# Hymba layer, second sweep: 32x32 vector transposes and a pass through DRAM in place of PE transposes for the keys of 14 chunks

## The chip, the core and the metric

The kernel runs on one core of one Trainium2 chip. The metric is the device time of one execution in microseconds (us). Engines are called PE (TensorE, matrix products), DVE (VectorE), ACT (ScalarE), POOL (GpSimd) and SP (SyncE, whose queue issues nearly all DMA transfers here). The on-chip memories are SBUF (128 partitions) and PSUM, where PE writes.

## The reference

One encoder layer on a sequence of 2048 rows of width 1024, in float32. One input projection feeds two groups of heads; their outputs are put side by side, go through one output projection, and a LayerNorm closes the layer. What the change touches is the second group, attention with compressed queries and keys:

```python
h = x @ w_in                        # split: GLA q,k,v,gate,ranks | c_q (256), c_kv (128), k_rope (64), gate
q  = (rms_norm(c_q,  q_norm_g)  @ w_uq ).reshape(B, S, 4, 128 + 64)
kv = (rms_norm(c_kv, kv_norm_g) @ w_ukv).reshape(B, S, 4, 128 + 128)
q_nope, q_rope = q[..., :128] * scale, apply_rope(q[..., 128:]) * scale
k_nope, v = kv[..., :128], kv[..., 128:]
k_r = apply_rope(k_rope)            # one rotary key for all heads
s = q_nope . k_nope + q_rope . k_r  # per head, 2048 x 2048
o = softmax(s) @ v
out = layer_norm(alpha * x + concat(gla * silu(gate_a), o * silu(gate_b)) @ w_out)
```

The first group is a gated linear attention with a forward and a backward scan over chunks of 64 rows.

## The kernel before

**Split products.** Each float32 operand is kept as a high part (a rounding copy to fp32r, `hi`, L353, mostly on ACT) and a low part (the difference, `lo`, L359, on DVE or POOL). A product is three matmuls: high by high, high by low, low by high (`mm3`, L407 to L409).

**Stages.** The sequence is cut into 16 chunks of 128 rows. A first sweep goes over the chunks from the last to the first and makes the projections of the linear attention and its backward scan (to about 340 us). The second sweep (`sweep_c`, about 359 to 589 us) goes forward in 8 steps of two chunks each. Then comes attention over 16 blocks (4 heads by 4 groups of 512 queries), and the output projection with the LayerNorm.

**The second sweep.** For each chunk PE makes `ipm` (c_q, c_kv and the rotary key); DVE and ACT make the RMS factor (`rm_t` to `rm_r`); ACT writes the normed `cq` and `ckv`, and high and low parts of `ckv` are kept as values, `vh` (ACT) and `vl` (POOL). The rotary key is made as `krs`, high and low halves of 64 columns side by side. The forward scan's output of the chunk is `Ob`, to which the first sweep's part `oib` is added; from it `rg_t` to `rg_r` make the norm's factor, `og` (DVE, with the state product `ub` that SP loads) the gated output, `oT` its transpose on DVE, and four SP transfers store it (`oa_s`). Once per step, PE makes the gates `pz`, from which ACT and DVE make `gm` (stored as `gm_s`), and the absorbed queries `pq`, split into `qah` and `qal` and stored as `qh_s` and `ql_s`; the rotary queries are stored as `rh_s` and `rl_s`. `pz`, `Ob` and `pq` share two PSUM buffers. SP loads the rows of x for a later step as `xcf`, which ACT splits to `xch` and POOL to `xcl`.

**The keys.** Scores need the keys with the feature on the partitions. `c_tm` (L1337 to L1341) transposes four 128x128 pieces per chunk on PE into one PSUM tile `tm`: two of `cq`, one of `ckv`, one of `krs`. From `tm`, ACT writes `ckvT_h` (high part of the transposed `ckv`), DVE writes `ckvT_l` (low part), and ACT writes the transposed `krs`. All three are tiles of 16 chunks that stay in SBUF for attention.

**The order.** Each piece of work of the sweep has a place: a number counted in steps, in tables (`PLACE_C`, `PLACE_C_FIRST` for the first step, `PLACE_C_LAST` for the last). All pieces are sorted by place and issued in that order; `in_order` chains the instructions of each engine, SP's transfers too, so that the order stays as written. Attention's loads are not in this chain: `fetch(i)` (L1515 to L1524) loads the queries of block i as six SP transfers, `qh`, `ql`, twice `rh`, twice `rl`, and a scheduler places those of the first blocks among the sweep's last SP transfers.

**Scores.** For each key tile PE runs five matmuls (L1534 to L1538), all into one PSUM bank:

```python
mm(ps[:, e], kh, qh, start=True, stop=False)
mm(ps[:, e], kh, ql, start=False, stop=False)
mm(ps[:, e], kl, qh, start=False, stop=False)
mm(ps[:, e], kr, rh, start=False, stop=False)
mm(ps[:, e], kr, rl, start=False, stop=True)
```

Here `kh`, `kl` and `kr` are slices of `ckvT_h`, `ckvT_l` and the transposed `krs`.

Of the kernel before, what the change touches and what calls it, by code (L numbers as in the profile page):

```python
# [9 lines left out]
F32 = mybir.dt.float32  # L10
F32R = mybir.dt.float32r
# [7 lines left out]
P = 128  # L19
# [3 lines left out]
NCH = S // P  # L23
# [8 lines left out]
NKT = S // P  # L32
# [97 lines left out]
SETUP_C = ("lset", "u15", "u14", "wS", "wH", "wL", "pb0", "wa0", "wh0", "wl0", "pb1", "wa1", "wh1", "wl1")  # L130
STEP_C = ("gm1", "gm2", "gm3", "gm4", "sgm", "pq", "qah", "qal", "sqa", "sqr")
CHUNK_C = ("lx", "xh", "xl", "lS", "lq", "lo", "lu", "sqm", "ssm", "rml", "rmd", "cq", "ckv", "krf", "krfa",
    "krsh", "krsl", "vh", "vl", "tm", "cqTh", "cqTl", "ckvTh", "ckvTl", "krT", "pqr", "qrf", "qrfa",
    "tq", "qrTh", "qrTl", "Sf1", "Sf2", "M", "Ob", "oib", "sqO",
    "ss", "rgl", "rgd", "og", "oT", "soT")

FETCH_C = ("lx", "xh", "xl")


PLACE_C = dict(  # L140
    ipa=(-0.08, 0.695),
    ipb=(-0.014, 0.701),
    ipc=(0.026, 0.723),
# [2 lines left out]
    tm=(0.532, 1.152),  # L146
    pqr=(0.849, 1.355),
# [6 lines left out]
    cq=(0.519, 1.042),  # L154
    ckv=(0.513, 1.1),
    vh=(0.732, 1.218),
    krsh=(0.45, 0.972),
    cqTh=(0.624, 1.184),
    ckvTh=(0.64, 1.277),
    krT=(0.848, 1.233),  # L160
# [9 lines left out]
    cqTl=(0.758, 1.284),  # L170
    ckvTl=(0.687, 1.321),
    qrf=(0.853, 1.411),
# [6 lines left out]
    krsl=(0.456, 1.044),  # L179
    vl=(0.859, 1.227),  # L180
    qrfa=(0.95, 1.459),
# [30 lines left out]
    wl1=0.556,  # L212
)
PLACE_C_FIRST = dict(
    ipa=(-1.874, 0.381),
    ipb=(-1.582, 0.655),
    ipc=(-0.643, 0.818),
# [2 lines left out]
    tm=(0.445, 1.143),  # L220
    pqr=(0.716, 1.336),
# [6 lines left out]
    cq=(0.33, 1.098),  # L228
    ckv=(0.414, 1.115),
    vh=(0.521, 1.151),  # L230
    krsh=(0.247, 0.988),
    cqTh=(0.547, 1.205),
    ckvTh=(0.483, 1.183),
    krT=(0.871, 1.252),
# [9 lines left out]
    cqTl=(0.579, 1.316),  # L244
    ckvTl=(0.54, 1.33),
    qrf=(0.968, 1.46),
# [6 lines left out]
    krsl=(0.252, 1.09),  # L253
# [89 lines left out]
class K:  # L343
# [145 lines left out]
    def run(self):  # L489
        tc, nc, ins = self.tc, self.nc, self.ins  # L490
        with ExitStack() as top:
            cp = top.enter_context(tc.tile_pool(name="const", bufs=1))
            self.cp = cp
            dp = top.enter_context(tc.tile_pool(name="scr", bufs=1, space=DRAM))
            self.qd_s = [dp.tile([P, H * P], F32, name=f"qd_s{c}") for c in range(NCH)]
            self.oi_s = [dp.tile([P, H * P], F32, name=f"oi_s{c}") for c in range(NCH)]
            self.su_s = [dp.tile([P, H * P], F32, name=f"su_s{c}") for c in range(NCH)]
            self.u_s = [dp.tile([P, H * P], F32, name=f"u_s{c}") for c in range(NCH)]
            self.qa_s = [[dp.tile([P, H, QB], F32, name=f"q{p}_s{b}") for p in "hl"] for b in range(NQB)]
            self.qr_s = [[dp.tile([H, 64, QB], F32, name=f"r{p}_s{b}") for p in "hl"] for b in range(NQB)]  # L500
            self.gm_s = [dp.tile([P, H, QB], F32, name=f"gm_s{b}") for b in range(NQB)]
            self.oa_s = [dp.tile([P, H, P], F32, name=f"oa_s{c}") for c in range(NCH)]
            self.qk_s = [[dp.tile([64, H, P], F32, name=f"{n}_s{c}") for c in range(NCH)] for n in ("qx", "kx")]
            self.r_s = [dp.tile([1, H, QB], F32, name=f"r_s{b}") for b in range(NQB)]
            self.ob_s = [dp.tile([P, H, QB], F32, name=f"ob_s{b}") for b in range(NQB)]

            ident = cp.tile([P, P], F32, name="ident")
            self.ident = ident
            self.gkv_c = cp.tile([P, 1], F32, name="gkv_c")
            self.gn_c = cp.tile([P, 1], F32, name="gn_c")  # L510
            self.cw = cp.tile([P, NCH, 3, H], F32, name="cw")

            psum = ExitStack()
            pspool = lambda n: psum.enter_context(tc.tile_pool(name=n, bufs=2, space=PSUM, reuse_waits="tile"))
            self.gp, self.ip, self.tr = pspool("gp"), pspool("ip"), pspool("tr")
            self.xfp = top.enter_context(tc.tile_pool(name="xfp", bufs=2, reuse_waits="tile"))
            edge = top.enter_context(tc.tile_pool(name="edge", bufs=1, side="right"))
            edge.tile([P, 8], F32, name="edge")
            self.keep = top.enter_context(tc.tile_pool(name="keep", bufs=1, side="right", reuse_waits="tile"))
            wgs = ExitStack()  # L520
            self.wgp = wgs.enter_context(tc.tile_pool(name="wgp", bufs=2 * NK + 1, side="right", reuse_waits="tile"))
            self.xab = wgs.enter_context(tc.tile_pool(name="xab", bufs=2, side="right"))
            self.wgate = []
            self.wl = None
            self.sweep_a()
            self.wz = top.enter_context(tc.tile_pool(name="wz", bufs=2 * NK + 1, reuse_waits="tile"))
            bcs = ExitStack()
            self.wm = bcs.enter_context(tc.tile_pool(name="wm", bufs=2 * NK + 1, reuse_waits="tile"))
            self.bc = bcs.enter_context(tc.tile_pool(name="bc", bufs=1, reuse_waits="tile"))
            self.wl = bcs.enter_context(tc.tile_pool(name="wl", bufs=2, reuse_waits="tile"))  # L530
            self.late_gates()
            wgs.close()
            rp = top.enter_context(tc.tile_pool(name="res", bufs=1, side="right", reuse_waits="tile"))
            self.ckvT_h = rp.tile([P, NKT, P], F32R, name="ckvT_h")
            self.ckvT_l = rp.tile([P, NKT, P], F32R, name="ckvT_l")
            self.kr = rp.tile([P, NKT, P], F32R, name="krs")
            self.vh = rp.tile([P, NKT, P], F32R, name="vh")
            self.vl = rp.tile([P, NKT, P], F32R, name="vl")
            self.sweep_c()
            bcs.close()  # L540
            psum.close()
            self.wof = top.enter_context(tc.tile_pool(name="wof", bufs=PRE_W, side="right", reuse_waits="tile"))
            self.attention()
# [565 lines left out]
    def sweep_c(self):  # L1109


        with ExitStack() as ctx:
            self.w1 = ctx.enter_context(self.tc.tile_pool(name="wk2", bufs=1, reuse_waits="tile"))
            self.sm = ctx.enter_context(self.tc.tile_pool(name="smc", bufs=2, reuse_waits="tile"))
            chunks = [dict(c=c, j=c % 2, st=c // 2) for c in range(NCH)]
            steps = [dict(st=st, ch=chunks[2 * st:2 * st + 2]) for st in range(NCH // 2)]
            for d in chunks:
                d["step"] = steps[d["st"]]
            self.Sf = None
            todo = []  # L1120

            def put(n, st, fn, *a, j=None):
                last = st == len(steps) - 1
                p = PLACE_C[n]
                p = (last and PLACE_C_LAST.get(n)) or (not st and PLACE_C_FIRST.get(n)) or p
                todo.append((st + (p if j is None else p[j]), len(todo), fn, a))

            for n in SETUP_C:
                put(n, 0, getattr(self, "su_" + n))
            for s in steps:  # L1130
                for n in range(8):
                    put("pz", s["st"], self.c_pz, s, n, j=n)
                for n in STEP_C:
                    put(n, s["st"], getattr(self, "c_" + n), s)
            for d in chunks:
                for n in range(4):
                    put("ip" + "abcd"[n], d["st"], self.c_ip, d, n, j=d["j"])
                for n in CHUNK_C:
                    if (d["st"] or n not in FETCH_C) and (d["c"] < NCH - 1 or n not in ("Sf1", "Sf2")):
                        put(n, d["st"], getattr(self, "c_" + n), d, j=d["j"])  # L1140
            last = dict(self.tail)
            for _, _, fn, a in sorted(todo, key=lambda e: e[:2]):
                with self.in_order(last):
                    fn(*a)
# [177 lines left out]
        self.nc.gpsimd.tensor_tensor(d["kr"], d["kr"], d["krt"], ALU.add)  # L1322

    def c_krsh(self, d):
        d["krs"] = self.w1.tile([P, 2, 64], F32R, tag="krs", name=f"krs{d['c']}")
        self.hi(d["krs"][:, 0], d["kr"][:, 0])

    def c_krsl(self, d):
# [5 lines left out]
    def c_vl(self, d):  # L1334
        self.lo(self.vl[:, d["c"]], d["ckv"], self.vh[:, d["c"]], "pool")

    def c_tm(self, d):  # L1337
        tp = d["tm"] = self.tr.tile([P, 4, P], F32, tag="tr", name=f"tm{d['c']}")
        for i, src in enumerate((d["cq"][:, 0:P], d["cq"][:, P:2 * P], d["ckv"],
                                 d["krs"].rearrange("p a d -> p (a d)").bitcast(F32))):  # L1340
            self.nc.tensor.transpose(tp[:, i], src, self.ident)  # L1341

    def c_cqTh(self, d):
        s = d["step"]
# [685 lines left out]
```

## Time and profile before

| what | value |
|---|---|
| time, median of 3 runs | 1277.12 us (1277.00 to 1278.61) |
| the profiled execution's own time | 1277.05 us |
| its span, first to last instruction | 1275.3 us |
| busy: PE / DVE / ACT / POOL | 1251.5 / 898.4 / 732.4 / 720.1 us |
| DMA | 155.24 MB, mean 122 GB/s |

In rows of the profile, "L1341 PE MATMUL tm<-ident,ckv" is the instruction of line 1341 on PE that writes tile `tm` from `ident` and `ckv`. In a timeline the first number is the start in us from the start of the span, the second the duration in us; a bracket holds the idle time of the engine just before, and what ended it. In a tile's rows the three numbers are the shortest, median and longest duration in ns; its last line has the time from the issue of its DMA transfers to their landing in us (shortest, median, longest). SPq is SP's queue: the rows are the issue of transfers. In a row of the windows stand the window, its length, the busy time of each engine with its number of instructions, PE's granted clock, the DMA engines' share and GB/s.

### The profile page before, as it was taken

Reading aid. Unit: us, or ns where it says so; the run is one execution under the profiler, and the core shown is the slowest. Engines: PE = TensorE matmul, PEld = TensorE weight load, DVE = VectorE, ACT = ScalarE, POOL = GpSimd, SP = SyncE. Lnnn points to the kernel's source line nnn. Section 1 sums busy time; section 2 is a strip of 40 time slices with the busy share of each in tenths; the row PEclk is TensorE's granted clock in tenths of the full one; section 3 lists DMA queues with packets and bytes.
Section 4 is the critical chain, followed back from the end, with each engine's and each line's share of the span. In section 5 each row is a group of like instructions: output and inputs, shape, how many; then the busy total and the mean of one; then the engine's idle time right before and its main releaser. Section 6 shows DMA issues by size and latency. Waiting matters only on the chain.

```text
span 1275.3 us, 19650 instructions
## 1 busy us (share of the span) xinstructions
PE 1251.5 (98%) x6986; PEld 1103.4 (87%) x6986; DVE 898.4 (70%) x1601; ACT 732.4 (57%) x1186; POOL 720.1 (56%) x443
## 2 busy tenths in 40 slices
PE   8999999999999999999999999999999999999997
PEld 7999999999899999989788888888888888887886
DVE  6635454544565555554888888888888888479997
ACT  7544444454565544544888888788888888511110
POOL 0132323232345555520598888889999999935541
PEclk9999999999999999999999999999999999999999
DMA  8223434334757777657201111111233110376652
GB/s 292 79 81 110 114 110 115 109 100 114 244 199 205 221 208 206 186 153 219 76 9 49 42 52 52 44 31 58 58 92 91 42 43 10 124 235 195 211 192 99
DMA packets 167233, 155.24 MB, mean 122 GB/s; under 512 B 77046, under 2 KB 119678, under 8 KB 167136
## 3 DMA queue, kind: packets, MB, share of 16 engines
q1 hardware_dynamic: 159072, 151.86, 40.0%
q0 software_dynamic: 672, 2.10, 0.4%
q8 instruction: 55, 0.90, 0.3%
q10 hardware_dynamic: 7392, 0.03, 0.3%
q14 instruction: 42, 0.34, 0.1%
HBM read 100.43 MB, written 53.51 MB: 121 GB/s over the span
## 4 chain that ended last, share of the span: by engine, by line
PE 84%; DVE 5%; DMA 4%; ACT 2%; issue 2%; SPq 2%; POOL 0%; DVEq 0%; ACTq 0%; POOLq 0%
PE pz L1217 7%; PE ipm L1288 5%; PE o L407 4%; PE o L408 4%; PE o L409 4%; PE pS L1534 4%; PE pS L1536 4%; PE pS L1537 4%; PE pS L1538 4%; PE pS L1535 4%; PE ipa L407 4%; PE ipa L409 4%; PE ipa L408 4%; PE ipg L407 2%; PE ipg L408 2%; PE ipg L409 2%
## 5 line engine op out<-in xcount | busy, mean ns | idle before, releaser
L359 POOL TENSOR_TENSOR pl<-s,ph 128x1024 fp32r<-128x1024 f32 x128 | 306.6, 2414 | 53.0 <-ACT ph L353 49.2
L1556 DVE TENSOR_TENSOR rm<-pS,rm 128x512 f32<-128x512 f32 x210 | 144.9, 690 | 35.7 <-ACT s L1543 30.4
L1543 ACT ACTIVATE s<-pS 128x1024 f32<-128x1024 f32 x128 | 131.2, 1025 | 60.6 <-PE pS L1538 51.4
L1580 DVE TENSOR_TENSOR s<-s,mb 128x1024 f32<-128x1024 f32 x128 | 151.2, 1214 | 9.5 <-PE mb L1574 8.8
L353 ACT ACTIVATE ph<-s 128x1024 fp32r<-128x1024 f32 x128 | 135.0, 1056 | 17.2 <-PE o L409 16.5
L1584 ACT ACTIVATE s<-s 128x1024 f32<-128x1024 f32 x128 | 131.3, 1049 | 11.0 <-DVE s L1580 10.9
L407 PE MATMUL ipa<-wah,xah 128*128 128x384 f32 (+1 forms) x384 | 130.1, 339 | 5.1 <-ACT wah L353 5.1
L408 PE MATMUL ipa<-wal,xah 128*128 128x384 f32 (+1 forms) x384 | 124.9, 325 | 0.0
L409 PE MATMUL ipa<-wah,xal 128*128 128x384 f32 (+1 forms) x384 | 124.7, 325 | 0.0
L1534 PE MATMUL pS<-qh,ckvT_h 128*128 128x512 f32 x256 | 102.5, 400 | 0.8 <-DVE rm L1556 0.4
L407 PE MATMUL o<-ph,vh 128*128 128x512 f32 x256 | 101.0, 395 | 0.0
L409 PE MATMUL o<-ph,vl 128*128 128x512 f32 x256 | 99.8, 390 | 0.0
L1537 PE MATMUL pS<-rh,krs 128*128 128x512 f32 x256 | 99.8, 390 | 0.0
L1536 PE MATMUL pS<-qh,ckvT_l 128*128 128x512 f32 x256 | 99.8, 390 | 0.0
L1538 PE MATMUL pS<-rl,krs 128*128 128x512 f32 x256 | 99.7, 389 | 0.0
L1535 PE MATMUL pS<-ql,ckvT_h 128*128 128x512 f32 x256 | 99.7, 389 | 0.0
L408 PE MATMUL o<-pl,vh 128*128 128x512 f32 x256 | 99.7, 389 | 0.0
L1054 POOL TENSOR_TENSOR Sb<-Sb,Us 64x512 f32<-64x512 f32 x15 | 20.9, 1394 | 137.0 <-DVE Us L1046 127.9
L1607 DVE TENSOR_TENSOR ap<-ap,s 128x512 f32<-128x512 f32 x120 | 83.1, 693 | 2.6 <-ACT s L1584 0.7
L407 PEld LDWEIGHTS ipa<-wah,xah 128*128 128x128 f32 x384 | 73.2, 191 | 7.8 <-ACT wah L353 5.5
L359 POOL TENSOR_TENSOR ol<-of,oh 128x512 fp32r<-128x512 f32 x32 | 43.4, 1357 | 64.0 <-ACT oh L353 63.3
L359 POOL TENSOR_TENSOR xal<-xaf,xah 128x1024 fp32r<-128x1024 f32 x12 | 29.7, 2477 | 87.8 <-ACT xah L353 87.8
(301 smaller groups left out, 3485.8 us busy)
## 6 DMA issues: line engine op xcount, KB each, us to landing
xcf<-xT_dram SPq DMA_DIRECT2D x16, 512.0 KB, 5.3
xr<-x_dram SPq DMA_DIRECT2D x16, 512.0 KB, 6.7
out_dram<-rr SPq DMA_DIRECT2D x32, 256.0 KB, 2.1
xaf<-xT_dram SPq DMA_DIRECT2D x14, 512.0 KB, 3.9
oib<-oi_s SPq DMA_DIRECT2D x16, 256.0 KB, 3.7
qdb<-qd_s SPq DMA_DIRECT2D x16, 256.0 KB, 3.4
SU<-su_s SPq DMA_DIRECT2D x16, 256.0 KB, 4.0
ub<-u_s SPq DMA_DIRECT2D x16, 256.0 KB, 3.9
```

The lines of the kernel that those rows point to most:

```text
L353: return nc.scalar.activation(dst, src, AF.Copy).ins
L359: return e.tensor_tensor(dst, src, hi.bitcast(F32), ALU.subtract).ins
L407: mm(out, ah, bh, start=start, stop=False)
L408: mm(out, ah, bl, start=False, stop=False)
L409: mm(out, al, bh, start=False, stop=stop)
L1534: mm(ps[:, e], kh, qh, start=True, stop=False)
L1535: mm(ps[:, e], kh, ql, start=False, stop=False)
L1536: mm(ps[:, e], kl, qh, start=False, stop=False)
L1537: mm(ps[:, e], kr, rh, start=False, stop=False)
L1538: mm(ps[:, e], kr, rl, start=False, stop=True)
L1556: V.tensor_tensor(d["rm"], src[:, e], d["rm"], ALU.max)
L1580: V.tensor_tensor(s, s, d["mb"][:, None, :].to_broadcast([P, 2, QB]), ALU.subtract)
```

## The change

For chunks 0 to 13 (steps 0 to 6), `ckv` and `krs` are no longer transposed by PE, and the three copies out of `tm` are left out. Instead DVE transposes `vh`, `vl` and `krs` of each chunk (`c_kvx`; three instructions, each of which transposes the 32x32 blocks of a 128x128 piece within their place). The result `kvx`, one buffer per step, is stored to a DRAM tile `kv_s` by four SP transfers per step (`c_skv`, 96 KB each, 768 runs of 128 bytes), which put the blocks in their order. Two calls of `kv_load` in the last step load the keys back to SBUF: chunks 0 to 11 by four SP transfers of 590 KB (1152 runs of 512 bytes each), chunks 12 and 13 by four of 96 KB. The three key tiles become one tile `kvT`, of which they are slices. `krs` gets a second buffer. The last step (chunks 14 and 15) stays as it was.

```diff
+LAST_C = ("ckvTh", "ckvTl", "krT")
+KV_LOADS = ((0, 12, 6.98), (12, 14, 7.99))
 PLACE_C = dict(
+    skv=1.65,
+    kvx=(1.02, 1.44),
...
 PLACE_C_FIRST = dict(
+    skv=1.66,
+    kvx=(0.95, 1.5),
...
+            self.kv_s = dp.tile([32, NCH, 3, 4, P], F32, name="kv_s")
...
-            self.ckvT_h = rp.tile([P, NKT, P], F32R, name="ckvT_h")
-            self.ckvT_l = rp.tile([P, NKT, P], F32R, name="ckvT_l")
-            self.kr = rp.tile([P, NKT, P], F32R, name="krs")
+            self.kvT = rp.tile([P, NKT, 3, P], F32R, name="kvT")
+            self.ckvT_h, self.ckvT_l, self.kr = (self.kvT[:, :, i] for i in range(3))
...
+                if s["st"] < len(steps) - 1:
+                    put("skv", s["st"], self.c_skv, s)
...
                 for n in CHUNK_C:
+                    late = d["st"] == len(steps) - 1
+                    if n in (LAST_C if not late else ("kvx",)):
+                        continue
...
+            for a, b, place in KV_LOADS:
+                todo.append((place, len(todo), self.kv_load, (slice(a, b),)))
...
-        d["krs"] = self.w1.tile([P, 2, 64], F32R, tag="krs", name=f"krs{d['c']}")
+        d["krs"] = self.w1.tile([P, 2, 64], F32R, tag="krs", name=f"krs{d['c']}", bufs=2)
...
+    def c_kvx(self, d):
+        s = d["step"]
+        if "kvx" not in s:
+            s["kvx"] = self.w1.tile([P, 2, 3, P], F32, tag="kvx", name=f"kvx{d['st']}")
+        for i, src in enumerate((self.vh[:, d["c"]], self.vl[:, d["c"]], d["krs"].rearrange("p a d -> p (a d)"))):
+            self.nc.vector.transpose(s["kvx"][:, d["j"], i], src.bitcast(F32))
+
+    def c_skv(self, s):
+        t = s["kvx"].rearrange("p a i (m t) -> p (a i m) t", m=4)
+        c = 2 * s["st"]
+        dst = self.kv_s[:, c:c + 2].rearrange("r a i m (b t) -> b r (a i m) t", b=4)
+        for b in range(4):
+            self.nc.sync.dma_start(dst[b], t[32 * b:32 * b + 32])
+
+    def kv_load(self, cs):
+        for m in range(4):
+            self.nc.sync.dma_start(self.kvT[32 * m:32 * m + 32, cs].rearrange("p c i t -> p (c i) t").bitcast(F32),
+                                   self.kv_s[:, cs, :, m].rearrange("r c i t -> r (c i) t"))
+
     def c_tm(self, d):
-        for i, src in enumerate((d["cq"][:, 0:P], d["cq"][:, P:2 * P], d["ckv"],
-                                 d["krs"].rearrange("p a d -> p (a d)").bitcast(F32))):
-            self.nc.tensor.transpose(tp[:, i], src, self.ident)
+        src = (d["cq"][:, 0:P], d["cq"][:, P:2 * P])
+        if d["st"] == NCH // 2 - 1:
+            src += d["ckv"], d["krs"].rearrange("p a d -> p (a d)").bitcast(F32)
+        for i, e in enumerate(src):
+            self.nc.tensor.transpose(tp[:, i], e, self.ident)
```

More of the change, by code (lines that the diff above doesn't have):

```diff
@@ L132 @@
 CHUNK_C = ("lx", "xh", "xl", "lS", "lq", "lo", "lu", "sqm", "ssm", "rml", "rmd", "cq", "ckv", "krf", "krfa",
-    "krsh", "krsl", "vh", "vl", "tm", "cqTh", "cqTl", "ckvTh", "ckvTl", "krT", "pqr", "qrf", "qrfa",
+    "krsh", "krsl", "vh", "vl", "kvx", "tm", "cqTh", "cqTl", "ckvTh", "ckvTl", "krT", "pqr", "qrf", "qrfa",
     "tq", "qrTh", "qrTl", "Sf1", "Sf2", "M", "Ob", "oib", "sqO",
```

## The prediction

> **What bounds the kernel now.** I read the page first (busy time, then the chain that ended last), then the windows of the second sweep, then the timelines of PE, VectorE (DVE), ScalarE (ACT) and SyncE's queue (SP) around the edit.
>
> ```profile
> PE 1251.5 (98%) x6986; PEld 1103.4 (87%) x6986; DVE 898.4 (70%) x1601; ACT 732.4 (57%) x1186; POOL 720.1 (56%) x443
> PE 84%; DVE 5%; DMA 4%; ACT 2%; issue 2%; SPq 2%; POOL 0%; DVEq 0%; ACTq 0%; POOLq 0%
> core 0: us, PE busy (x) PEld busy (x) DVE busy (x) ACT busy (x) POOL busy (x), PEclk, DMA share, GB/s
> 416.28:444.82 28.54, 28.54 (x211) 27.79 (x210) 15.17 (x56) 14.22 (x40) 15.01 (x16) 1.00 0.73 213
> 587.50:612.00 24.50, 23.23 (x114) 19.25 (x112) 14.52 (x20) 13.46 (x15) 2.44 (x3) 1.00 0.79 233
> ```
>
> PE is busy 98% of the span and makes 84% of the chain. One step of the sweep (the fourth row) is all PE: 28.54 of 28.54 us, DVE, ACT and POOL half idle, the DMA engines at 0.73. So PE work taken out of a step is worth its own time, as long as no other engine's result then comes too late; and each us that PE waits is a us lost, in attention too (last row, its first 24.5 us: PE 23.23 busy). The profiled run took 1277.05 us, 1.75 more than its span, and lies 0.07 under the median of three runs (1277.12). The sum is made on 1277.05. About 0.2%, 2.55 us, is what a measurement of this kernel can tell from no change.
>
> **Part 1: the transposes that leave PE.** Rows of PE's timeline at chunk 11, and of the tiles involved:
>
> ```profile
> 530.06 0.27 PE L1341 MATMUL tm<-ident,ckv 128*128 128x128 f32 x1
> 530.17 0.27 PE L1341 MATMUL tm<-ident,krs 128*128 128x128 f32 x1
> 530.20 0.36 PE L1217 MATMUL pz<-xch,wzh 128*128 128x256 f32 x1
> 528.21 1.13 DVE L1458 SCALAR_TENSOR_TENSOR og<-Ob,rg_r,ub 128x128 f32<-128x128 f32 x4
> L359 DVE TENSOR_TENSOR ckvT_l<-tm,ckvT_h x16: 281/283/292, 372.1 to 587.6; 128x128 fp32r<-128x128 f32 x16
> L1464 DVE STREAM_TRANSPOSE oT<-og x16: 711/712/715, 376.7 to 572.9; 128x512 f32<-128x512 f32 x16
> ```
>
> On PE a transpose lasts 0.27 us but starts 0.11 us after the one before (530.17 minus 530.06), so two cost 0.22 us a chunk and 28 cost 3.1 us. The 28 ACT copies and 14 DVE subtractions that go are at nothing: both engines are idle half of each step.
>
> In their place DVE gets 42 transposes of 128x128. The trace has none of that size. From below, a quarter of the 128x512 one is 0.18 us; from above, the 128x128 subtraction is 0.28. I take 0.24, between the two, because both are DVE passes of nearly this shape: 0.72 us for a chunk's three (0.53 to 0.85). In the built order the even chunk's three stand ahead of `rg_t` to `og` of the odd chunk of its step, which must be done before the next step's `pz` (PE's wait for it is in the rows of part 3). `og` ends at 529.34 (528.21 + 1.13), `pz` starts at 530.20: a cover of 0.86. The odd chunk's dropped transposes, just ahead of `pz`, pull it forward by 0.22, so 0.64 is left, against 0.72. Of the odd chunk's saving some 0.1 us then stays (the new `og` end is 530.06, and it takes a moment to be seen); the even chunk's 0.22 stays whole. Seven even chunks and six odd ones make **minus 2.1 us**. Chunk 13's share is hidden, as PE waits 2.07 us soon after it (part 3). The best end is minus 2.9.
>
> The Trainium skill ("VectorE: DVE Perf Modes", "Rules for kernel authors") says to transpose 128x128 on TensorE where the result may go to PSUM, and its table of the three transpose paths puts DVE's 128x128 (bf16) at 311 ns, in 32x32 blocks only. By that figure a chunk's three would last 0.93 us, an estimate, and the even half would turn into a loss of 0.2 us a step; the trace's rows of DVE lie lower, and I go by them.
>
> **Part 2: four more stores a step on SP.** They stand between a `ub` load and the next `xcf` load.
>
> ```profile
> 514.14 0.64 SPq L1396 DMA_DIRECT2D ub<-u_s  x1
> 514.87 1.11 SPq L473 DMA_DIRECT2D xcf<-xT_dram  x1
> 524.26 1.05 ACT L353 ACTIVATE xch<-xcf 128x1024 fp32r<-128x1024 f32 x1
> L1470 SPq DMA_DIRECT2D oa_s<-oT x64: 573/631/1042, 384.1 to 593.7; - x64
> DMA to landing us min/median/max: 5.1/5.4/5.6
> ```
>
> The nearest row is `oa_s`, also stores of 128-byte runs out of a DVE transpose, 512 runs where a `kv_s` store has 768: 0.63 us to issue each, 0.95 scaled by runs, so 2.5 to 3.8 us for four. `xcf` then goes out at 517.4 to 518.7 and, with its own landing time (last row, 5.4), is there at 522.8 to 524.1; ACT takes it at 524.26. I cost it at nothing, with a cover of 0.2 to 1.5 us. If the cover goes, ACT's `krs`, the `og` copy and the chain of part 1 stand behind it: up to 1 us a step, 6 us in all.
>
> **Part 3: the first load back, in the last step.** SP gets four `kvT` loads of 590 KB, 1152 runs each, between the two `oib` loads.
>
> ```profile
> 555.46 1.05 SPq L1396 DMA_DIRECT2D oib<-oi_s  x2
> 560.16 0.62 SPq L1396 DMA_DIRECT2D ub<-u_s  x1
> 562.30 1.16 PE L1435 MATMUL Ob<-SU,qdb 128*128 128x128 f32 x8 [2.07 <-DVE og L1458]
> 566.48 1.13 DVE L1458 SCALAR_TENSOR_TENSOR og<-Ob,rg_r,ub 128x128 f32<-128x128 f32 x4
> 572.95 0.39 PE L1217 MATMUL pz<-xch,wzh 128*128 128x256 f32 x1 [0.20 <-DVE og L1458]
> DMA to landing us min/median/max: 2.9/3.4/3.8
> ```
>
> In the built order each SP transfer also waits for the one eight places before it, so `ub` of chunk 14 waits for the third `kvT` load. Three of them carry 1.77 MB. At the 213 to 233 GB/s of the windows above that takes 7.6 to 8.3 us, from about 556.5 (issued behind the first `oib`) to 564.5; with some start-up, I say 565. `ub` then lands at 568.5 to 569 (last row, 3.4), and `og`, which read it at 566.48, starts **2.5 us** late. Before, PE waited for just this tile's chain (the rows with brackets), so nothing hides it. Bounds: 0.5, where the loads run faster than the windows' mean, and 5, where their small pieces halve the rate. Chunk 13's three DVE transposes stand on the same chain ahead of the last `og`, at which `pz` waits: **plus 0.7**.
>
> **Part 4: what the new SP order does to attention's first loads.** This is the largest term, and the diff doesn't show it: the first block's loads of `ql`, `rh` and `rl` are placed by the scheduler, and in the built order they have moved past the last `gm_s`, `oa_s`, `rh_s`, `rl_s`, `qh_s` and `ql_s` stores of step 7.
>
> ```profile
> 581.29 0.56 SPq L1520 DMA_DIRECT2D ql<-ql_s  x1
> 581.95 1.13 SPq L1524 DMA_DIRECT2D rh<-rh_s  x2
> 583.17 1.19 SPq L1524 DMA_DIRECT2D rl<-rl_s  x2
> ...
> 590.60 0.58 SPq L1238 DMA_DIRECT2D gm_s<-gm  x1
> 591.24 3.10 SPq L1470 DMA_DIRECT2D oa_s<-oT  x4
> ...
> 597.18 0.58 SPq L1259 DMA_DIRECT2D ql_s<-qal  x1
> 590.54 0.39 PE L1538 MATMUL pS<-rl,krs 128*128 128x512 f32 x1
> 589.35 1.23 DVE L1231 TENSOR_TENSOR gm<-pz,gm 128x1024 f32<-128x1024 f32 x1 [1.46 <-ACT gm L1228]
> DMA to landing us min/median/max: 2.8/3.9/4.3
> ```
>
> Before, `ql`, `rh` and `rl` go out at 581.29 to 584.36, and PE reads `rl` at 590.54. SP then holds the queue for `gm`, which DVE makes at 589.35, and the stores run to 597.76. In the new order `ql` can go out only there. With the same issue times (0.56, then 1.13 for two `rh`, and half of 1.19), the second `rl` load starts at about 600.2 and lands, with 4.3 (the last row is the tile `rl`), at 604.5. PE's first score needs all four tiles, PE runs in order and nothing else stands ahead of the scores: it stops for 604.5 minus 590.54, **plus 13.9 us**. Part 3's delay moves the `gm` chain and PE alike, so the gap keeps its length. Bounds: 12 (landing 2.8, a shorter issue) and 16 (the loads' lanes are held by the stores ahead). Nothing gives it back: attention's windows are all PE. The second kv load, issued ahead of those stores, lands before `rl` does and is hidden behind it.
>
> **Part 5: the clock after the stop.** PE has no long stop between its first matmul and its last in the trace; the nearest case is the start of the span.
>
> ```profile
> 5.14 0.61 PE L407 MATMUL ipa<-wah,xah 128*128 128x288 f32 x1 [5.14 <-ACT wah L353]
> 10.55 0.44 PE L407 MATMUL ipa<-wah,xah 128*128 128x288 f32 x1
> 10.79 0.44 PE L408 MATMUL ipa<-wal,xah 128*128 128x288 f32 x1
> 11.34 0.29 PE L408 MATMUL ipa<-wal,xah 128*128 128x288 f32 x1
> 11.47 0.29 PE L409 MATMUL ipa<-wah,xal 128*128 128x288 f32 x1
> 1270.00:1275.30 5.30, 0.00 (x0) 0.00 (x0) 2.11 (x7) 0.00 (x0) 0.00 (x0) 0.56 0.27 99
> ```
>
> From 5.14 to about 11.0 matmuls of one size follow each other every 0.24 us, later every 0.13: 5.9 us at half pace, 2.9 us lost. At the end, some us after PE's last matmul, the granted clock is down to 0.56. So a stop of 14 us should lower it. I take **plus 2.0**, between 0 (PE's clock holds) and 3, nearer to the start's row. The Trainium skill ("TensorE: Matmul & The Clock Gate", "Part 1: The HAM clock gate") says that the clock halves after an idle window of some 3.4 us and returns after some 3.4 us of work; by that the loss would be 1.7 us, an estimate, and the sum 0.3 less.
>
> **Sum.** Minus 2.1, plus 2.5, plus 0.7, plus 13.9, plus 2.0 is plus 17.0: 1277.05 + 17.0 = **1294.1 us**. All low ends (minus 2.9, 0.5, 0.5, 12, 0) give plus 10.1, 1287; the high ends (plus 4 where `xcf` is late in six steps, 5, 0.9, 16, 3) plus 28.9, 1306.
>
> **Rivals.**
> Faster: the first block's loads come in time after all. For that the last `rl` load must be issued before about 586 (590.54 minus 4.3), which takes an SP order other than the one I read, or a `gm` that is ready 15 us earlier. For it speaks that SP is idle from 586 to 590.6. Against it stands `gm` at 589.35, which must be stored first. Then parts 4 and 5 fall away, and if the `kvT` loads also land before `ub` is due, it is minus 2.1 to 2.9: 1274.5.
>
> No difference: the loads come in time, but part 3 stands: minus 2.1, plus 2.5, plus 0.7 is 1278.2, inside 0.2%.
>
> Slower still: `xcf` lands late in each step, because 393 KB of 128-byte pieces lengthen the landings at a DMA share that is 0.73 already. It decides once the four stores take more than 4 us of the queue, and costs about 1 us in each of six steps on top: 1294.1 + 6 + the lost 2.1 = 1302.
>
> The change does what it says in any case: the built program has 28 fewer PE transposes, 42 more on DVE and 28 stores and 8 loads where the text puts them.
>
> **How the numbers follow.** The forecast (the first score waits for `rl`) 0.80, the slower rival 0.09, no difference 0.05, faster 0.06. The forecast's own range is 1287 to 1301; leaving out the two rivals on the low side and part of the slow one, 8 in 10 lie in 1286 to 1302. Faster by over 0.2%: 0.06; within: 0.05; slower: 0.89.
>
> **What would show it.** In the profile after: PE idle at its first or second score for 12 to 16 us, released by the DMA of `ql`, `rh` or `rl`; these loads behind the last `ql_s` in SP's timeline; some us of granted clock near 0.5 right after; `og` of chunk 14 some 2.5 us later against the start of its step; steps of 28.2 instead of 28.54 us. The prediction is wrong if PE goes from `pq` to the scores without a stop, or if a step grows.

## The result, and the profile after

The changed kernel takes 1306.97 us (median of 4 runs, 1306.16 to 1307.62), the kernel before 1277.86 us beside it: slower by 2.25% (ratio 1.0225, 95% interval 1.021 to 1.024), 29.1 us. The forecast was slower, 1294.1 us, with 1286 to 1302 as its range. The direction and the largest term were right; the time lies outside the range.

The profiled run of the changed kernel has a span of 1304.9 us, 29.6 us longer. First the page: busy time and the chain that ended last.

```profile
PE 1256.0 (96%) x6958; PEld 1106.4 (85%) x6958; DVE 905.6 (69%) x1629; ACT 728.6 (56%) x1158; POOL 719.5 (55%) x443
PE 82%; DVE 6%; DMA 4%; ACT 3%; SPq 3%; issue 1%; POOL 0%; DVEq 0%; ACTq 0%; POOLq 0%
```

PE does 28 instructions less and yet is busy 4.5 us longer, at 96% instead of 98%: it works part of the time at half pace, and it waits more. What it waits for, between 340 and 640 us (total, times, longest):

```profile
PE pS L1570 <- DMA ql<-ql_s: 12.9, 1, 12.9
PE pq L413 <- DVE og L1493: 10.1, 1, 10.1
PE Ob L1470 <- DVE og L1493: 2.9, 1, 2.9
PE pz L1230 <- DVE og L1493: 1.2, 3, 0.8
```

In the kernel before, the longest wait in this stretch was 2.1 us at `Ob`, the next 1.3 us. Now there are two long stops, one in the last step and one right behind it. The windows of the last step and of attention's start show the granted clock (the column after POOL) falling with them:

```profile
530.44:559.00 28.56, 28.36 (x204) 27.54 (x205) 14.91 (x53) 12.24 (x32) 12.55 (x15) 1.00 0.69 192
559.00:587.50 28.50, 15.51 (x83) 14.37 (x83) 14.92 (x56) 6.33 (x21) 4.09 (x5) 0.76 0.90 166
587.50:612.00 24.50, 15.42 (x130) 15.06 (x128) 6.82 (x20) 8.06 (x22) 2.92 (x6) 0.91 0.66 166
```

In the second window PE is busy for 15.51 of 28.50 us, where it was 25.53 before, and the DMA share is up from 0.62 to 0.90.

The timeline of SP's queue tells the first stop, with DVE's and PE's rows beside it:

```profile
555.70 0.43 SPq L1431 DMA_DIRECT2D oib<-oi_s  x1
556.17 8.02 SPq L1367 DMA_DIRECT2D kvT<-kv_s  x4
564.30 3.01 SPq L1431 DMA_DIRECT2D oib<-oi_s  x1
567.35 5.01 SPq L1505 DMA_DIRECT2D oa_s<-oT  x4
572.40 1.63 SPq L1251 DMA_DIRECT2D gm_s<-gm  x1
574.08 0.63 SPq L1431 DMA_DIRECT2D ub<-u_s  x1
...
577.93 1.12 DVE L1493 SCALAR_TENSOR_TENSOR og<-Ob,rg_r,ub 128x128 f32<-128x128 f32 x4 [10.88 <-DMA ub<-u_s]
579.11 0.58 PE L413 MATMUL pq<-cqT_h,wabs_h 128*128 128x256 f32 x1 [10.09 <-DVE og L1493]
DMA to landing us min/median/max: 7.6/11.5/12.8
```

The four `kvT` loads take 8.02 us to issue, everything behind them is held, and `ub` of chunk 14 goes out at 574.08 where it went out at 560.16. (The last row is the landing of these four loads. Taken one by one they are issued at 556.17, 556.68, 557.62 and 560.94, and land at 563.8, 567.1, 570.3 and 573.7: one behind the other, some 3.3 us apart.)

The second stop is the one that part 4 forecast:

```profile
603.51 0.56 SPq L1251 DMA_DIRECT2D gm_s<-gm  x1
604.12 3.09 SPq L1505 DMA_DIRECT2D oa_s<-oT  x4
...
610.16 0.58 SPq L1272 DMA_DIRECT2D ql_s<-qal  x1
610.84 0.98 SPq L1555 DMA_DIRECT2D ql<-ql_s  x1
...
615.85 0.79 PE L1570 MATMUL pS<-ql,kvT 128*128 128x512 f32 x1 [12.93 <-DMA ql<-ql_s]
618.29 0.76 PE L1573 MATMUL pS<-rl,kvT 128*128 128x512 f32 x1 [0.47 <-DMA rl<-rl_s]
```

`ql` goes out behind the last store, some 8 us after PE first asks for it, and lands 5.0 us later. Between 615.85 and 620.99 the score matmuls are 0.63 us long and 0.43 apart; then 0.39 long and 0.23 apart.

### The profile page after: what moved, and what is told of

It is laid out like the page before. It is cut to its first block, busy times and chain, and to the rows that moved or that the text cites. A ratio compares the mean times of both kernels' runs of the same rounds, so it can differ in the third digit from the quotient of the medians.

```text
span 1304.9 us, 19622 instructions
## 1 busy us (share of the span) xinstructions
PE 1256.0 (96%) x6958; PEld 1106.4 (85%) x6958; DVE 905.6 (69%) x1629; ACT 728.6 (56%) x1158; POOL 719.5 (55%) x443
## 4 chain that ended last, share of the span: by engine, by line
PE 82%; DVE 6%; DMA 4%; ACT 3%; SPq 3%; issue 1%; POOL 0%; DVEq 0%; ACTq 0%; POOLq 0%
PE pz L1230 7%; PE pS L1573 4%; PE o L413 4%; PE o L414 4%; PE pS L1569 4%; PE o L415 4%; PE pS L1571 4%; PE pS L1572 4%; PE pS L1570 4%; PE ipa L413 4%; PE ipa L415 4%; PE ipa L414 4%; PE ipm L1301 3%; PE ipg L413 2%; PE ipg L414 2%; PE ipg L415 2%
## 5 line engine op out<-in xcount | busy, mean ns | idle before, releaser
L1570 PE MATMUL pS<-ql,kvT 128*128 128x512 f32 x256 | 100.4, 392 | 12.9 <-DMA ql<-ql_s 12.9
L1569 PE MATMUL pS<-qh,kvT 128*128 128x512 f32 x256 | 102.9, 402 | 0.8 <-DVE rm L1591 0.4
L1573 PE MATMUL pS<-rl,kvT 128*128 128x512 f32 x256 | 100.4, 392 | 0.5 <-DMA rl<-rl_s 0.5
L1572 PE MATMUL pS<-rh,kvT 128*128 128x512 f32 x256 | 100.5, 393 | 0.0
L1571 PE MATMUL pS<-qh,kvT 128*128 128x512 f32 x256 | 100.3, 392 | 0.0
```

## The experiments

All kernels build on the changed one. Times are medians of their own job, with the kernel before on the same chip beside them (1277.1 to 1277.6 in these jobs).

**e1: the first block's loads ahead of the stores.** The six loads are issued inside the sweep's own order.

```diff
+            todo.append((8.05, len(todo), self.fetch_q, (0,)))   # qh, ql, rh x2, rl x2 of block 0
 ...
-            fetch(0)
+            stt[0]["q"] = self.q0
```

> The first block's six query loads are pinned in SP's order behind the second kv load and ahead of the stores of chunk 14, as they stood before the change; all else as after. Theory (the loads wait behind the stores): PE's 12.9 us wait for ql and 0.5 us for rl go, and with them the some 2.5 us of half-pace matmuls behind that stop; block 0 waits about 1 us more for its maximum, as before the change. 1307.0 - 13.4 - 2.5 + 1 = 1292. Rival (the loads are not the limit, the first score would wait for the key loads or for the queue anyway): PE still stops at the first scores for 5 us or more, 1297 to 1307.

Measured: 1290.63 us (ratio to before 1.0101, 1.0086 to 1.0116), 16.3 us less than the changed kernel. No wait for `ql` or `rl` is left, and `pq`'s wait for `og` is still 10.2 us:

```profile
PE pq L413 <- DVE og L1505: 10.2, 1, 10.2
PE Ob L1482 <- DVE og L1505: 3.6, 1, 3.6
```

So the second stop is the order of these loads alone, and with the half pace behind it costs 16 us.

**e2: the same bytes in longer runs.** The DRAM tile is laid out so that a load reads 3 KB at a time.

```diff
-            self.kv_s = dp.tile([32, NCH, 3, 4, P], F32, name="kv_s")
+            self.kv_s = dp.tile([NCH // 2, 32, 4, 2, 3, P], F32, name="kv_s")
-        t = s["kvx"].rearrange("p a i (m t) -> p (a i m) t", m=4)
+        t = s["kvx"].rearrange("p m a i t -> p (m a i) t")
```

> The kv loads carry the same bytes in the same place, but in runs of 3 KB instead of 512 bytes (the first four have 192 runs each instead of 1152); DVE writes kvx in another order of columns for that, the stores keep 768 runs of 128 bytes. Theory (the number of pieces holds SP's queue in the last step): the four issues take about 2 us instead of 8.0, ub of chunk 14 goes out near 562 instead of 574.1, PE's 10.1 us wait for og shrinks to 0 to 2 and the half pace behind it goes: 1307.0 - 9 - 2.5 = 1295.5, 1293 to 1298. Rival (the bytes hold it: 2.36 MB at some 220 GB/s are 10.7 us in any case): the wait stays at 8 us or more, 1304 to 1308.

Measured: 1307.53 us (ratio to before 1.0234, 1.0219 to 1.025); the rival holds. SP's queue:

```profile
556.45 0.44 SPq L1430 DMA_DIRECT2D oib<-oi_s  x1
556.93 2.42 SPq L1366 DMA_DIRECT2D kvT<-kv_s  x4
559.45 0.66 SPq L1430 DMA_DIRECT2D oib<-oi_s  x1
560.15 10.20 SPq L1504 DMA_DIRECT2D oa_s<-oT  x4
570.39 3.31 SPq L1251 DMA_DIRECT2D gm_s<-gm  x1
573.75 0.63 SPq L1430 DMA_DIRECT2D ub<-u_s  x1
```

The four issues went from 8.02 to 2.42 us as expected, but the time came back at once: `oa_s` takes 10.20 instead of 5.01 us, `gm_s` 3.31 instead of 1.63, and `ub` goes out at 573.75, as late as before. Cutting the number of pieces to a sixth brought nothing.

**e3: both edits.** The edits of e1 and e2 together.

> Both edits of the two runs before in one kernel. If the two waits are independent, the gains add: 1307.0 - 15 - 11.5 = 1280.5, and PE has no stop over 4 us between 559 us and the first scores' end. If one only hides the other, it stays at the better of the two alone, some 1292.

Measured: 1288.28 us (1.0089, 1.0066 to 1.0111). e1's gain, and 2.4 us on top, which overlaps the scatter of the two; the gains don't add up to the 1280.5 us of the first case, since `pq` still waits 9.5 us for `og`. It is the base of the next runs.

**e4: the even chunk's DVE transposes behind `og`.**

```diff
-    kvx=(1.02, 1.44),
+    kvx=(1.115, 1.44),
```

> As e3, and the even chunk's three DVE transposes stand behind og and oT of the odd chunk instead of ahead of them (place 1.115 instead of 1.02). Theory (the sweep's saving is lost since og, at which pz waits, is late by the three transposes): pz's waits for og (0.82 us in the step of chunk 11) go, each of steps 0 to 6 gets up to 0.4 us shorter, e3 - 2.5 us. Rival (the saving is lost elsewhere, by slower stores or loads): within 0.5 us of e3.

Measured: 1286.35 us (1.0073, 1.0057 to 1.0089), 1.9 us under e3, with overlapping intervals. The profile is sharper than the times: from chunk 1's `tm` to chunk 13's it is 170.89 us, in e3 172.14, in the changed kernel 172.50, in the kernel before 172.49. What the earlier place costs is to be seen in the changed kernel, in the step of chunk 11:

```profile
527.85 0.31 DVE L1356 STREAM_TRANSPOSE kvx<-vh 128x128 f32<-128x128 f32 x1
528.09 0.27 DVE L1356 STREAM_TRANSPOSE kvx<-vl 128x128 f32<-128x128 f32 x1
528.28 0.27 DVE L1356 STREAM_TRANSPOSE kvx<-krs 128x128 f32<-128x128 f32 x1
529.46 1.12 DVE L1493 SCALAR_TENSOR_TENSOR og<-Ob,rg_r,ub 128x128 f32<-128x128 f32 x4 [0.28 <-DVE rg_r L435]
530.64 0.39 PE L1230 MATMUL pz<-xch,wzh 128*128 128x256 f32 x1 [0.82 <-DVE og L1493]
```

`og` starts 1.25 us later than before the change (528.21), ends at 530.58, and `pz` waits 0.82 us for it.

**e5: the first kv loads behind the last `ub`.**

```diff
-KV_LOADS = ((0, 12, 6.98), (12, 14, 7.99))
+KV_LOADS = ((0, 12, 7.48), (12, 14, 7.99))
```

> As e3, with the first four kv loads placed behind the ub load of chunk 15 instead of ahead of oib of chunk 15 (place 7.48 instead of 6.98): same bytes, same runs, some 10 us later in SP's order, no load of the sweep behind them. Theory (oa_s, gm_s and ub wait in SP's queue for the landing of the first, second and third kv load, 11 to 15 us, and PE waits for ub): PE's waits for og at pq (9.5 us) and the half pace after it go, 1288.3 - 9.5 - 1.5 = 1277.5, 1276 to 1279.5. Rival (2.4 MB in the last step slow down whatever runs beside them, wherever they stand): the wait shows again, at oib or ub or at the first scores, 1284 to 1289.

Measured: 1283.68 us (1.005, 1.0036 to 1.0063), 4.6 us under e3 where 10.8 were expected. The wait at `pq` is gone, but a new one has come, at chunk 15's `tm`. The rows of SP, ACT and PE:

```profile
575.10 8.60 SPq L1363 DMA_DIRECT2D kv_s<-kvx  x4
583.80 1.06 SPq L1279 DMA_DIRECT2D rh_s<-qrTh  x2
...
586.77 0.38 ACT L359 ACTIVATE qrTh<-tq 128x256 fp32r<-128x256 f32 x1 [6.54 <-DMA rh_s<-qrTh]
587.05 0.36 ACT L1329 ACTIVATE ckv<-ipm,rm_r 128x128 f32<-128x128 f32 x1
587.46 0.47 PE L1387 MATMUL tm<-ident,ckv 128*128 128x128 f32 x1 [4.79 <-ACT ckv L1329]
```

The `kv_s` stores, 2.7 to 5.2 us in the changed kernel, take 8.60 us behind the loads (issued from 565.71); `rh_s` goes out late, ACT's next `qrTh` waits 6.54 us for its buffer, and `ckv` stands behind it. My theory was right on where the first wait comes from, the rival on where it goes.

**e6: the loads spread over steps 3 to 7.**

```diff
+KV_LOADS = ((0, 6, 3.91), (6, 8, 4.91), (8, 10, 5.91), (10, 12, 6.91), (12, 14, 7.99))
```

> As e3, with the kv loads spread over steps 3 to 7, each behind the rl_s stores (chunks 0 to 5 in step 3, then two chunks a step): 1.2 MB in step 3, 0.4 MB in each later one, ahead of oib of chunk 15 too. Theory: landings of 0.4 MB stay under 5 us, og in the last step is at most 2 us late, 1288.3 - 9 - 1.5 = 1278; a loss of up to 2 us in step 3. Rival (four more transfers ahead of oib and ub cost by their number, not by their bytes): the last step's wait for og stays over 6 us, 1284 or more.

Measured: 1281.22 us (1.0029, 1.002 to 1.0038), 3 us more than expected. The last step's long wait is gone with four transfers still ahead of `oib` and `ub`, so it goes by bytes. The 1.2 MB in one step cost PE 2.6 us there (a wait for POOL's `qrf`, 473 to 502 us).

**e7: as e6, with e4's place.**

> As e6, with the even chunk's DVE transposes behind og as in e4. e4 was 1.9 us under e3 with steps 0 to 6 shorter by 1.25 us, so 1278 - 1.9 = 1276, 1274.5 to 1278: at best 0.2% under the kernel before. If the two edits meet in the queue, no gain over e6.

Measured: 1280.24 us (1.0025, 1.0014 to 1.0036), 4 us more than expected: the wait in step 3 (2.3 us) stayed, and in the last step `oib`, behind a load, is late (`Ob` waits 2.75 us for `og`).

**e8: no keys of chunks 0 to 13.** No transposes of them, no stores, no loads; POOL fills the tile (`memset`) once.

> Leaves out the keys of chunks 0 to 13 altogether: no PE transposes of them, no DVE transposes, no stores, no loads; POOL fills the key tile once. The first block's loads stand as in e1. It is what the change could save at most. Theory (a transpose takes 0.11 us of PE's time and PE is the bound): steps 0 to 6 shorter by 0.4 us each, 1277.2 - 3.0 = 1274. Rival (PE's other waits take the place of the transposes): within 1 us of the kernel before.

Measured: 1273.57 us (0.9973, 0.9962 to 0.9983), 3.8 us under the kernel before (2.2 to 4.9 by the interval). From chunk 1's `tm` to chunk 13's it is 169.81 us, 2.68 less than before: 0.45 for each of six steps, the four transposes' 0.44. The transposes are worth what part 1 priced; that is the most that this change could bring.

**e9: the loads spread evenly, none ahead of the last step's `ub`.**

```diff
+KV_LOADS = ((0, 2, 1.91), (2, 4, 2.91), (4, 6, 3.91), (6, 8, 4.91), (8, 10, 5.91), (10, 14, 7.99))
```

> As e7, with the loads spread evenly: two chunks in each of steps 1 to 5 (393 KB a step), none ahead of the ub loads of the last step, and chunks 10 to 13 together where chunks 12 and 13 were loaded. e7 lost 2.3 us of PE in the step whose load was 1.2 MB (PE waits for qrf of POOL) and 0.7 us more than the kernel before at og in the last step. Theory (a load costs only where its landing outlasts the room behind it): both go, 1280.2 - 3 = 1277.2, 1275.5 to 1278.5. Rival (the DMA engines, 0.8 to 0.9 busy in each step, are the limit wherever the loads stand): 1280 or more.

Measured: 1276.95 us against 1277.06 (1.0000, 0.9991 to 1.0008), as expected. PE's only wait over 1 us from 340 to 640 us is 3.0 us at `Ob`. The DMA share is 0.83 to 0.90 in the steps, and PE is still full in four of the five steps read (the second row is the fifth):

```profile
473.36:501.90 28.54, 28.54 (x210) 27.80 (x209) 16.47 (x61) 13.70 (x37) 14.95 (x16) 1.00 0.90 239
501.90:530.44 28.54, 27.76 (x201) 26.81 (x201) 16.03 (x59) 13.20 (x36) 14.90 (x16) 1.00 0.88 237
```

Of the 2.7 us that e8 saves up to chunk 13's `tm`, this version keeps 1.2 (171.32 us from chunk 1's `tm`, 172.49 before). It loses 2.6 from there to the first score (32.54 us, 29.91 before): PE waits 0.9 us longer at `Ob`, runs at half pace behind it (granted clock 0.50 from 562 to 564 us), and waits 0.8 us for chunk 15's `ckv`.

**e10: as e9, with the odd chunk's transposes behind the last `og`.**

> As e9, with the odd chunk's three DVE transposes behind og of chunk 15 in the last step too (place 1.52 instead of 1.44). PE's wait of 0.5 us for that og at pz goes: e9 - 0.5 us, against no change if ub is what og waits for.

Measured: 1276.94 us (0.9994, 0.9985 to 1.0003): no difference to e9 or to the kernel before that these runs can tell. The waits at `pz` went from 0.8 to 0.5 us and at `Ob` from 3.0 to 2.0, below what the times show. From chunk 1's `tm` to chunk 13's it takes 171.39 us, from there to the first score 31.54. e9 and e10 are the best versions found; neither beats the kernel before.

**e11: half the bytes.** The first four loads carry chunks 0 to 5; the keys of chunks 6 to 11 are left out.

```diff
-KV_LOADS = ((0, 12, 6.98), (12, 14, 7.99))
+KV_LOADS = ((0, 6, 6.98), (12, 14, 7.99))
```

> The changed kernel with half the bytes in the first four kv loads: chunks 0 to 5 (288 KB each, 576 runs of 512 bytes), in the same place; leaves out the keys of chunks 6 to 11, which POOL fills once. Theory (ub waits for landings, and these go by bytes): the stretch from the first kv load's issue to ub's (556.2 to 574.1 in the changed kernel) gets some 6.5 us shorter, PE's 10.1 us wait for og shrinks to 3 to 4 us: 1307.0 - 6.5 - 1.5 = 1299. Rival (the wait goes by the number of transfers and their order): 1306 to 1307.

Measured: 1300.45 us (1.0178, 1.0162 to 1.0193). The stretch from the loads' issue to `ub`'s:

```profile
555.15 2.95 SPq L1372 DMA_DIRECT2D kvT<-kv_s  x4
...
567.08 0.62 SPq L1436 DMA_DIRECT2D ub<-u_s  x1
PE pq L413 <- DVE og L1498: 4.2, 1, 4.2
```

11.9 us instead of 17.9, and 4.2 us of wait instead of 10.1. The same number of transfers in the same order: the wait goes by bytes. (The runs are halved too, but e2 showed that their number doesn't matter here.)

**e12: the loads issued from POOL's queue.** As e3, with `self.nc.gpsimd.dma_start` for the first four loads; no transfer of SP waits for them.

> As e3, with the first four kv loads issued from POOL's queue instead of SP's, at the same place of the sweep: the same 2.36 MB at the same time, but no transfer of SP's waits for their landing. Theory (the order in SP's queue holds ub, through the waits on transfers eight places back): ub of chunk 14 goes out within 2 us of oib plus 5 as before the change, PE's wait for og at pq falls from 9.5 us to 0 to 3, and 1288.3 - 8 - 1.5 = 1279, up to 1282 if POOL's own work behind the issue gets late. Rival (the DMA engines are full, and ub lands late whoever issues the loads): the wait stays over 6 us, 1285 or more.

Measured: 1287.78 us (1.0079, 1.0061 to 1.0097), against e3's 1288.28: the rival holds.

```profile
556.00 2.32 POOL L1378 DMA_DIRECT2D kvT<-kv_s  x4
561.65 0.64 SPq L1442 DMA_DIRECT2D ub<-u_s  x1
575.17 1.13 DVE L1504 SCALAR_TENSOR_TENSOR og<-Ob,rg_r,ub 128x128 f32<-128x128 f32 x4 [7.89 <-DMA ub<-u_s]
576.35 0.58 PE L413 MATMUL pq<-cqT_h,wabs_h 128*128 128x256 f32 x1 [6.90 <-DVE og L1504]
DMA to landing us min/median/max: 13.4/13.4/13.4
```

`ub` went out at 561.65, 8.1 us after the first `oib` (4.7 before the change, 18.4 in the changed kernel), and landed 13.4 us later (last row) instead of 3.4. PE's two waits, here 5.2 us at `Ob` and 6.9 at `pq`, are 12.1 us in all; in e3 they were 3.2 and 9.5, 12.7 in all. So the order in SP's queue, on which I put the delay, is only the form that it took. The DMA engines had 2.36 MB in hand, and `ub` waited for them either ahead of its issue or behind it.

## Why the prediction was wrong, point by point

The span grew by 29.6 us. Read from the same instructions in both traces (chunk 13's `tm` on PE at 559.63 and 559.85; the first score at 589.54 and 602.45; block 0's maximum, `mx`, at 611.49 and 639.69; the end at 1275.3 and 1304.9):

| stretch | forecast | measured |
|---|---|---|
| to chunk 13's `tm` (parts 1, 2) | minus 2.1 | plus 0.2 |
| to the first score (part 3) | plus 3.2 | plus 12.7 |
| to block 0's maximum (parts 4, 5) | plus 15.9 | plus 15.3 |
| to the end | 0 | plus 1.4 |

**Part 1: the price right, the cover misread.** e8 shows 0.45 us a step for the PE transposes. DVE's three transposes put off the next instruction by 0.74 us (`rg_t` starts 0.81 us behind `rm_r`, before 0.07), as priced (0.72). But the forecast kept the even chunk's half in every step. From one odd chunk's `tm` to the next, the first five stretches take 28.62, 28.43, 28.52, 28.33 and 28.19 us (before 28.54 each, in e8 28.1), and the sixth, from chunk 11 to 13, takes 30.41 (before 29.79, in e8 29.34). Together that is nothing saved (172.50 against 172.49). The cover of `og` was read as 0.86 us against one step's rows; in the step of chunk 11 `og` started 1.25 us later, 0.74 of it from the transposes, 0.20 from within the norm's chain and 0.31 from ACT's late `xch` (part 2), and `pz` waited 0.82 us, more than the 0.44 saved. With the transposes behind `og` (e4), 1.6 of the 2.7 us came back. Nearly all of the other 1.1 is in the first and the sixth stretch (28.61 and 29.79 us in e4): `pz` starts 0.64 and 0.58 us behind `tm` there and 0.14 in e8, still behind `og`. For the first, e4's edit left the transposes where they were (`PLACE_C_FIRST`); why `og` is late in the sixth is open. One estimate of the prediction doesn't add up: at 0.93 us for three transposes, the forecast's own cover of 0.64 leaves 0.29 us of delay against 0.44 saved in a step, not a loss of 0.2.

**Part 2: put at nothing, and nearly so.** SP's four stores took 2.67 to 5.23 us a step, where 2.5 to 3.8 were forecast. In the step of chunk 11 the cover was gone:

```profile
514.66 5.23 SPq L1363 DMA_DIRECT2D kv_s<-kvx  x4
519.99 0.47 SPq L479 DMA_DIRECT2D xcf<-xT_dram  x1
524.57 1.06 ACT L359 ACTIVATE xch<-xcf 128x1024 fp32r<-128x1024 f32 x1 [0.65 <-DMA xcf<-xT_dram]
```

`xch` starts 0.31 us later than before (524.26), and the chain up to `og` moves by the same 0.31. No other step waits for `xcf`.

**Part 3: the step that failed.** The chain was named rightly (loads, `ub` of chunk 14, `og`, PE), and its size was wrong. `og` of chunk 14 was forecast 2.5 us late, with an upper bound of 5; it starts at 577.93 instead of 566.48, 11.2 us late counted from chunk 13's `tm`. The term that failed is the landing of the loads: the forecast gave 1.77 MB the windows' whole 213 to 233 GB/s and had the third load landed by 565, and it landed at 570.3. From the first issue to the last landing the four loads took 17.6 us for 2.36 MB, 134 GB/s, while the core's DMA moved 196 GB/s in all (556 to 574 us): what the page gives as GB/s is the sum with the rest, and the rest doesn't stop. Behind the loads the forecast counted no time for the queue, but `oib`, `oa_s` and `gm_s` took 3.01, 5.01 and 1.63 us to issue, and `ub` went out at 574.08 instead of 565.

Counted from the first `oib`'s issue, `ub` has landed after 22.2 us in the changed kernel (574.08 + 3.8 - 555.70), 21.5 in e12 (575.05 - 553.57) and 16.3 in e11 (567.08 + 3.8 - 554.60); before the change it was some 8 (560.16 + 3.4 - 555.46 = 8.1). So 2.36 MB put it off by 14 us and half of that by 8: more bytes, more delay, though not in a fixed ratio. The bound of 5 us for small pieces was the wrong bound too, since runs of 3 KB changed nothing (e2). The waits for transfers eight places back, on which the forecast rested, are not needed for the delay (e12).

The last 1.7 of the 12.7 us are the clock, which part 5 counted for the second stop alone: from 579.11 on, `pq` matmuls last 0.41 us and start 0.21 apart, where those before the change lasted 0.28 and started 0.12 apart, and from `pq` to `pz` it is 6.73 us instead of 5.04. Two readings were off without weight: the 2.07 us wait at `Ob` before the change was for chunk 13's `og`, held by `oib`, while chunk 14's `og` ended 0.3 us ahead of `pq` (567.61 and 567.91); and the 0.7 for chunk 13's DVE transposes didn't show, as `pz` starts at 585.84, 0.97 us behind the end of the last `og`.

**Part 4: right.** 12.9 us at `ql` and 0.5 at `rl`, 13.4 against 13.9; e1 takes just these away. Most of the wait fell on `ql` rather than on `rl`, since `ql` took 5.0 us to land, more than the 4.3 taken for `rl`.

**Part 5: right.** The nine score matmuls from 615.85 to 620.99 took 4.7 us without the stop for `rl`, at 0.23 apart they would take 2.0: 2.6 us, forecast 2.0 with an upper end of 3. The rule of the Trainium skill ("TensorE: Matmul & The Clock Gate", "Part 1: The HAM clock gate") would make it 1.7: the trace's 4.7 us at half pace are longer than its 3.4, and shorter than the 5.9 at the span's start (where the profile's clock column shows 1.00). Its idle window of some 3.4 us does not bound the stop either: one of 2.00 us was enough in e10 (see the last section). Block 0's own waits for its maximum fell from 1.3 to 0.3 us in exchange.

**The last 1.4 us are open.** From `mx` to the end it is 663.8 us before and 665.2 after, but between 663.1 (e9) and 665.5 (e3) in the other kernels, whose code is the same there; it is as much as runs differ.

**The rivals.** None of the three came true. The slow one came nearest in time (1302) and had the wrong place, `xcf` in the steady steps, where it shows in one step with 0.3 us. By its own terms the forecast's upper end without that rival is 1300, not 1301 (minus 2.1, 5, 0.9, 16 and 3 on 1277.05).

The rule of the Trainium skill against this change ("VectorE: DVE Perf Modes", "Rules for kernel authors": transpose 128x128 on TensorE) is borne out here: 28 transposes at 0.11 us of PE's time each are 3.1 us, leaving them out gives back 3.8 (e8), and the best arrangement of the other way gives back nothing that can be measured (e10). That page's 311 ns for DVE's transpose ("The three transpose paths") are near the 0.27 to 0.31 us that the rows show for float32, though these start 0.19 to 0.24 apart.

## What to carry to other kernels

A load that is moved into a stage where the DMA engines are 0.6 to 0.9 busy is not over after its bytes divided by the GB/s of the page, since that rate is taken already: here that gives 10 to 11 us for 2.36 MB, and the loads took 17.6. What is issued behind them or beside them lands late too, in this kernel from either queue. Spread such loads over the steps (e9), and keep the last ones out of the way of what the next stage reads first. And after any edit to a queue, read the built order for transfers that are not in the edit: here the largest single loss, 16 us, was of six loads that the diff doesn't name, and pinning them (e1) took it away.

## What was not expected of the hardware

Cutting the loads' pieces to a sixth cut the time to issue them from 8.02 to 2.42 us but hardly their landing (the last at 573.3 instead of 573.7) and not the kernel's time (e2). Loads from POOL's queue delayed a load from SP's queue by 10 us (3.4 to 13.4 us to land, e12), at a DMA share of 0.97 from 556 to 575 us: the second queue was no shield here.

The length of a stop alone does not say whether PE's clock falls. Behind the stop at `Ob` in the last step it fell to 0.50 after 2.00 us (e10), 2.44 (e8), 2.90 (the changed kernel) and 2.96 (e9), and held at 1.00 after 2.07 (before), 2.38 (e2), 2.75 (e7) and 3.21 us (e4). The windows behind it in e10 and in e4:

```profile
562.00:564.00 2.00, 1.87 (x6) 1.08 (x5) 1.79 (x11) 1.29 (x6) 1.63 (x3) 0.50 0.67 100
562.00:564.00 2.00, 1.37 (x8) 0.98 (x6) 1.90 (x10) 1.05 (x5) 0.67 (x2) 1.00 1.00 203
```

What decides it is open.
